# Casts at the beginning, norm 2's plain product and the products of the end, rearranged in a decoder block kernel

## The chip, the cores and the metric

The kernel runs on one core of a Trainium2 chip. The metric is device microseconds of one execution: the median of 3 runs of the kernel before is 800.8 us (800.53 to 800.96). One more execution was profiled.

## What is computed

A decoder block on 512 tokens of 1024 channels, in float32. Two token mixers, a causal convolution and a recurrence, are merged by gates; a channel mixer follows. Cut to what the change touches:

```python
h = rmsnorm(x, norm1_g)                     # norm 1
z = h @ w_in + b_in                         # 1024 -> 6656 columns
...
x = x + m @ w_mix_out
h = rmsnorm(x, norm2_g)                     # norm 2
x = x + (silu(h @ ffn_w1) * (h @ ffn_w3)) @ ffn_w2
return rmsnorm(x, norm_f_g)                 # final norm
```

## The kernel before

Every product of two float32 matrices is made of three matmuls of a rounded type: each operand is split into a high part (a cast) and a low part (the operand less its high part), and high x high, high x low and low x high are added up. `split_to` (line 114) makes such a pair: line 123 the cast, line 119 the subtraction. Weights come in chunks of 128x1024: `emit_chunk` (line 145) issues the load on SP's queue (`raw_in` for w_in), casts on ScalarE, and subtracts on GpSimd or VectorE into `hl_in`. Tokens are split into two halves, LO and HI, of 256.

The program has four engines with orders of their own. In the block of lines 595 to 618 the order of TensorE, ScalarE, VectorE and SP is that of the code; elsewhere a scheduler picks it, within the limits that `tc.issue_after` sets. On each engine, instructions run in that order.

**Beginning.** TensorE first runs WARM products of a matrix of ones (line 495). Of x, each of four token tiles t has two column halves; `norm1_rows(t)` squares them on ScalarE (lines 539, 545), takes the root (546) and the reciprocal (547), and scales x on VectorE (579). The small per-channel parameters are loaded as rows (`load_rows`) and transposed into `par` (`rows_turned`, line 507, and a copy, 508). `turn_half("tx", ...)` transposes a token half of x on TensorE (563), ScalarE casts it, scaled by the norm's gain, to the high parts h10h to h17h (566), and VectorE makes the low parts h10l to h17l (567). `early_mm(i, half)` multiplies four chunks of weights, numbers 0, 8, 1 and 9 of w_in (the first to fourth that are loaded), by these (`mm3`, line 523, tile z).

**Norm 2.** `turn_half("th", ...)` does the same for h20 to h27. Token half LO is turned early, and the products fr of it run meanwhile (`f_product`, line 1060). Then half HI is turned (the four th pieces around 472 us), and the plain products of the feed-forward network, f1 and f3 of column blocks 0 and 11, run over all 512 tokens (`mm3`, line 523, tile f). `ffn_out` takes silu of f1 (ScalarE, line 1051, tile si) and multiplies by f3 (VectorE, line 1052, ou and ov). All other blocks go through a scheme with seven products instead of eight, for which sums of weights are formed (VectorE, line 351, tile raw_fb; GpSimd stores them by DMA, line 349, and SP loads them, line 339), and sums of h2: `full` (line 1067) adds a high and a low part to h2f (VectorE, line 886, tile hf), and `f_inputs` makes hs from it. `f_out` (line 1115) ends a block: silu on ScalarE (line 1117, with a table load), and a product on VectorE (1118).

**End.** `out_end` (line 1199) finishes four token tiles. `finish` (line 1181) takes the root of the mean square (`rstd_begin`, `rstd_end`, tiles jk) and scales by it and by the gain gf to `of`, two DMAs for each tile. For the last two tiles a lambda, `third`, makes the last products (tile or, line 933).

## Time and profile before

| | us |
| --- | --- |
| median of 3 runs | 800.8 |
| profiled execution, its own time | 800.93 |
| its span in the trace | 799.2 |
| TensorE busy | 788.9 |
| VectorE busy | 675.5 |
| ScalarE busy | 472.1 |
| GpSimd busy | 231.6 |

In the profile PE is TensorE's matmuls, DVE is VectorE, ACT is ScalarE, POOL is GpSimd and SP the engine that issues most DMAs. A row gives a start, a length, the engine, the line of the kernel, the operation, output and inputs, shape and count; in square brackets stands how long the engine had been idle and what ended that. A 512-column matmul is 0.39 us long on its own, but pipelined ones start closer together, so what one costs is read from start to start.

### The profile page before, as it was taken

The numbers are of one execution on the slowest core, as the hardware profiler recorded it, in microseconds if no ns is written. First come the engines' busy times: TensorE is split into PE (matmuls) and PEld (weight loads), VectorE is DVE, ScalarE is ACT, GpSimd is POOL, SyncE is SP. The second block draws the span as 40 slices with busy tenths as digits, with TensorE's granted clock in tenths as the row PEclk, the third lists the DMA queues.
The fourth block names the chain that finished last, engine by engine and source line by source line (L and its number), as shares of the span: only waits on it lengthen the run. The fifth ranks groups of instructions, "written<-read, shape, count | busy, mean of one in ns | idle before, by whom it ended". The sixth has DMA issues, their size and how long they took to land.

```text
span 799.2 us, 12191 instructions
## 1 busy us (share of the span) xinstructions
PE 788.9 (99%) x4374; PEld 689.5 (86%) x4374; DVE 675.5 (85%) x1027; ACT 472.1 (59%) x678; POOL 231.6 (29%) x182
## 2 busy tenths in 40 slices
PE   8999999999999999999999999999999999999997
PEld 7988888888888888888888888999999999888885
DVE  4699899999989988796787889978778887889756
ACT  7546595898668855563335574545455555577443
POOL 3565867687766855130000000000000000000000
PEclk9999999999999999999999999999999999999999
DMA  7945647378564754468947536477555553676552
GB/s 212 239 122 165 174 150 212 121 213 237 164 193 144 225 177 125 128 193 266 282 153 246 172 107 183 120 178 190 147 132 133 133 132 106 205 265 203 198 172 105
DMA packets 184624, 140.29 MB, mean 176 GB/s; under 512 B 14279, under 2 KB 162163, under 8 KB 184563
## 3 DMA queue, kind: packets, MB, share of 16 engines
q1 hardware_dynamic: 183123, 134.27, 55.4%
q0 software_dynamic: 1440, 5.24, 3.5%
q8 instruction: 34, 0.56, 0.3%
q14 instruction: 27, 0.22, 0.1%
HBM read 113.79 MB, written 18.64 MB: 166 GB/s over the span
## 4 chain that ended last, share of the span: by engine, by line
PE 91%; DVE 4%; DMA 2%; ACT 2%; issue 1%; SPq 0%; DVEq 0%; POOLq 0%; ACTq 0%
PE z L523 35%; PE or L933 13%; PE ft L1060 7%; PE yb L523 7%; PE fa L1060 6%; PE ya L523 5%; PE mxr L933 5%; PE fe L1060 3%; PE g L807 3%; PE fr L1060 3%; PE fb L1060 2%; PE f L523 1%; DMA raw_fb<-in_ffn_w_dram 1%; DMA raw_fb<-raw_fb 1%; DMA x<-in_x_dram 1%
## 5 line engine op out<-in xcount | busy, mean ns | idle before, releaser
L682 DVE SCALAR_TENSOR_TENSOR cv<-u,par,cv 128x511 f32<-128x511 f32 (+16 forms) x240 | 162.0, 728 | 2.3 <-ACT cv L679 2.2
L119 POOL TENSOR_TENSOR hl_in<-raw_in,hl_in 128x1024 fp32r<-128x1024 f32 x52 | 125.9, 2426 | 82.8 <-ACT hl_in L123 80.4
L349 POOL DMA_DIRECT2D raw_fb<-raw_fb x10 | 8.7, 874 | 299.3 <-DVE raw_fb L351 186.6
L119 POOL TENSOR_TENSOR ows<-ows 128x256 f32<-128x256 f32 x66 | 57.2, 870 | 37.5 <-DMA ows<-in_ffn_w_dram 34.5
L123 ACT CAST hl_in<-raw_in 128x1024 fp32r<-128x1024 f32 x52 | 54.2, 1043 | 10.2 <-PE z L523 6.5
L123 ACT CAST hl_ft<-raw_fb 128x1024 fp32r<-128x1024 f32 x40 | 41.8, 1048 | 28.9 <-DVE raw_fb L351 12.7
L119 DVE TENSOR_TENSOR hl_ft<-raw_fb,hl_ft 128x1024 fp32r<-128x1024 f32 x40 | 48.6, 1219 | 9.7 <-ACT hl_ft L123 9.6
L119 DVE TENSOR_TENSOR hl_fb<-raw_fb,hl_fb 128x1024 fp32r<-128x1024 f32 x30 | 36.6, 1220 | 9.2 <-ACT hl_fb L123 8.9
L523 PE MATMUL z<-h10h,hl_in 128*128 128x512 f32 (+1 forms) x112 | 42.2, 378 | 1.0 <-DVE h10l L567 1.0
L523 PE MATMUL z<-h13h,hl_in 128*128 128x512 f32 (+1 forms) x112 | 41.7, 374 | 0.0
L523 PE MATMUL z<-h14h,hl_in 128*128 128x512 f32 (+1 forms) x112 | 41.7, 374 | 0.0
L523 PE MATMUL z<-h15h,hl_in 128*128 128x512 f32 (+1 forms) x112 | 41.7, 374 | 0.0
L523 PE MATMUL z<-h11h,hl_in 128*128 128x512 f32 (+1 forms) x112 | 41.7, 374 | 0.0
L523 PE MATMUL z<-h16h,hl_in 128*128 128x512 f32 (+1 forms) x112 | 41.7, 374 | 0.0
L523 PE MATMUL z<-h17h,hl_in 128*128 128x512 f32 (+1 forms) x112 | 41.7, 374 | 0.0
L523 PE MATMUL z<-h12h,hl_in 128*128 128x512 f32 (+1 forms) x112 | 41.7, 374 | 0.0
L351 DVE TENSOR_TENSOR raw_fb<-raw_fb,raw_fb 128x1024 f32<-128x1024 f32 x20 | 24.5, 1225 | 16.9 <-DMA raw_fb<-in_ffn_w_dram 16.6
L119 DVE TENSOR_TENSOR hl_ob<-raw_ob,hl_ob 128x1024 fp32r<-128x1024 f32 (+1 forms) x23 | 27.0, 1172 | 10.5 <-ACT hl_ob L123 7.6
L123 ACT CAST hl_ob<-raw_ob 128x1024 fp32r<-128x1024 f32 (+1 forms) x23 | 23.4, 1016 | 20.7 <-PE or L933 14.7
L123 ACT CAST hl_fb<-raw_fb 128x1024 fp32r<-128x1024 f32 x30 | 31.4, 1047 | 6.7 <-PE mxr L933 3.7
L1060 PE MATMUL fe<-hs_0h,hl_ft 128*128 128x256 f32 x160 | 30.8, 284 | 0.4 <-DVE hl_ft L119 0.4
L1060 PE MATMUL ft<-hs_1h,hl_ft 128*128 128x256 f32 x160 | 30.4, 283 | 0.0
(965 smaller groups left out, 2610.1 us busy)
## 6 DMA issues: line engine op xcount, KB each, us to landing
raw_in<-in_w_in_dram SPq DMA_DIRECT2D x52, 512.0 KB
raw_fb<-in_ffn_w_dram SPq DMA_DIRECT2D x96, 256.0 KB
ows<-in_ffn_w_dram SPq DMA_DIRECT2D x44, 256.0 KB
os<-ows SPq DMA_DIRECT2D x22, 512.0 KB
raw_ob<-in_ffn_w_dram SPq DMA_DIRECT2D x33, 256.0 KB
raw_ot<-os SPq DMA_DIRECT2D x33, 256.0 KB
raw_lo<-in_lru_w_out_dram SPq DMA_DIRECT2D x16, 320.0 KB
raw_fb<-raw_fb POOLq DMA_DIRECT2D x10, 512.0 KB, 4.5
```

Of the source, the lines that this page charges most:

```text
L119: return eng.tensor_tensor(out=o, in0=x, in1=y, op=ALU.subtract)
L123: copy(h, full)
L349: pool_e.dma_start(out=q, in_=y, accum_op=ALU.add)
L351: vec.tensor_tensor(out=q, in0=q, in1=y, op=ALU.add)
L523: pe.matmul(ps, l, r, start=i == 0, stop=i == n - 1)
L682: vec.scalar_tensor_tensor(out=acc[c][:, s:], in0=u[c][:, : T - s], scalar=dw(c, s), in1=acc[c][:, s:], op0=ALU.mult, op1=ALU.add)
L807: pe.matmul(ps, l, r, start=k == 0, stop=k == len(mms) - 1)
L933: pe.matmul(banks[i], l_[:, ts], r_, start=start and n == 0, stop=stop and n == 2, skip_group_check=again)
L1060: pe.matmul(ps[:, HALVES[i]], lw[:, 4 * i + c, :], rx_, start=not (again or i or c or m), stop=bool(i and c == 3 and m == 2), skip_group_c ...
```

## The change

At the beginning, WARM goes from 12 to 21; the first four chunks of weights are cast by VectorE (`vec.tensor_copy`) instead of ScalarE; the second chunk's cast comes behind the low parts of the first half on VectorE, and the third's and fourth's ahead of the second half's; the parameter rows other than norm 1's gains are loaded behind x, and turned later, in a matrix of rows of their own.

At norm 2, the token half HI is turned in four portions of two pieces. ScalarE first copies a piece to h2f (scaled, in full), then casts that, and VectorE subtracts; the additions of `full` for HI go. Behind each portion stands a quarter of the plain product f1 of block 0: LO with rows 0 to 3 of h2, LO with 4 to 7, then HI likewise, in matmuls of 256 columns. The f3 of that block makes its low parts last. `f_out` of the first blocks waits until the last copy to h2f has been issued.

At the end, `finish` is split: `finish_begin` makes the square of x2's second half and its product with the gain for both of the last two tiles ahead of the last products; the scaling of that product goes to VectorE for all but the very last tile.

```diff
--- before.py
+++ after.py
@@ -34,7 +34,7 @@
 RAW = 4
 HL = 5
 AHEAD = 4
-WARM = 12
+WARM = 21
 
 FEW, MANY = 32, 112
 
@@ -128,11 +128,11 @@
             last = sub(eng, l, full, h.bitcast(F32))
         if eng is pool_e:
             newest["sub"] = last.ins
-        return h, l
+        return h, l, last
 
     def split(name, full, eng, p_=None, copy=act.copy):
         p_ = p_ or pairt(name)
-        return split_to(*p_, full, eng, copy)
+        return split_to(*p_, full, eng, copy)[:2]
 
 
     chunks = []
@@ -142,7 +142,7 @@
     def wchunk(key, src, kt, cols, where="hl", lo=pool_e, after=None):
         chunks.append((key, src, kt, cols, where, lo, after))
 
-    def emit_chunk():
+    def emit_chunk(copy=act.copy):
         if emitted[0] == GATES_AT:
             load_gates()
         key, src, kt, cols, where, lo, after = chunks[emitted[0]]
@@ -161,7 +161,7 @@
             newest["load"] = nc.sync.dma_start(rv.rearrange("p (k n) -> p k n", k=kt), src).ins
         if where != "long":
             hl = hls.tile([P, 2, 1024], F32R, tag="hl", name=f"hl_{key}")
-            h, l = split_to(hl[:, 0, :n], hl[:, 1, :n], rv, lo)
+            h, l, _ = split_to(hl[:, 0, :n], hl[:, 1, :n], rv, lo, copy)
             if after:
                 after(rv, h)
             held[key] = (h.rearrange("p (k n) -> p k n", k=kt), l.rearrange("p (k n) -> p k n", k=kt))
@@ -171,9 +171,9 @@
                 for i in range(2)
             ]
 
-    def emit_to(n):
+    def emit_to(n, copy=act.copy):
         while emitted[0] < min(len(chunks), n):
-            emit_chunk()
+            emit_chunk(copy)
 
     def weights(key, ahead=AHEAD):
         i = next(i for i, c in enumerate(chunks) if c[0] == key)
@@ -452,7 +452,12 @@
     n_rows = sum(n for _, n in ROWS)
     n_first = ROWS[0][1] + ROWS[1][1]
     par = consts.tile([P, n_rows], F32, name="par")
-    row_at = lambda c: (0, c) if c < n_first else (1 + (c - n_first) // P, (c - n_first) % P)
+    starts = (0, ROWS[0][1], n_first)
+
+    def row_at(c):
+        b = sum(c >= s_ for s_ in starts) - 1
+        return b + (c - starts[b]) // P, (c - starts[b]) % P
+
     at, col, parts = 0, {}, []
     for name, n in ROWS:
         col[name] = at
@@ -497,8 +502,7 @@
     first = [i for i, (lo, _, _) in enumerate(parts) if lo < n_first]
     load_x(0)
     load_x(1)
-    for i in first:
-        load_rows(i)
+    load_rows(first[0])
 
     def rows_turned(c0, c1):
         pt = bank2(f"par_ps{c0}")
@@ -553,7 +557,7 @@
             between()
         return rstd_end(begun, halves[1], junk[1])
 
-    def turn_half(name, rows, gname, dest, hf, bk, some=range(ND)):
+    def turn_half(name, rows, gname, dest, hf, bk, some=range(ND), full=None):
 
         cs = slice(hf * 256, hf * 256 + 256)
         for c in some:
@@ -563,6 +567,11 @@
                 pe.transpose(ps[:, t * P : (t + 1) * P], src, ident)
             g = pc(gname, c)
             h, l = (v[:, cs] for v in dest[c])
+            if full:
+                f = full[c][:, cs]
+                newest["half"] = act.activation(f, ps[:, :256], AF.Copy, scale=g).ins
+                _, _, last = split_to(h, l, f, vec)
+                continue
             act.activation(h, ps[:, :256], AF.Copy, scale=g)
             last = vec.scalar_tensor_tensor(out=l, in0=ps[:, :256], scalar=g, in1=h.bitcast(F32), op0=ALU.mult, op1=ALU.subtract)
         return last.ins
@@ -595,24 +604,26 @@
     with tc.manual_schedule(engines={ET.PE, ET.Activation, ET.DVE, ET.SP}):
         norm1_rows(0)
         norm1_rows(1)
-        rows_turned(0, n_first)
-        emit_to(1)
+        rows_turned(0, ROWS[0][1])
+        emit_to(1, vec.tensor_copy)
         turn_half("tx", xt, "norm1_g", h1p, 0, [bank, bank, bank, bank2])
-        emit_to(2)
+        emit_to(2, vec.tensor_copy)
         load_x(2)
         load_x(3)
+        for i in first[1:]:
+            load_rows(i)
         norm1_rows(2)
         norm1_rows(3)
-        emit_to(3)
+        emit_to(4, vec.tensor_copy)
         for i in range(len(parts)):
             if i not in first:
                 load_rows(i)
         early_mm(0, 0)
         early_mm(1, 0)
         turn_half("tx", xt, "norm1_g", h1p, 1, [bank2, bank, bank])
-        emit_to(4)
         early_mm(2, 0)
         early_mm(3, 0)
+        rows_turned(ROWS[0][1], n_first)
         rows_turned(n_first, n_rows)
         for i in range(4):
             early_mm(i, 1)
@@ -1073,8 +1084,17 @@
 
     for c in range(ND):
         full(c, LO)
-    turned = turn_half("th", xs, "norm2_g", h2p, 1, [bank2])
     h2 = parts_of(h2p)
+    plain_1 = bank(f"f1_{PLAIN}")
+    with tc.manual_schedule(engines={ET.PE}):
+        ws = w_tiles(f"f1_{PLAIN}", ND, 0)
+        for q in range(4):
+            cs, ks = HALVES[q // 2], range(4 * (q % 2), 4 * (q % 2) + 4)
+            turned = turn_half("th", xs, "norm2_g", h2p, 1, [bank2], range(2 * q, 2 * q + 2), h2f)
+            for k in ks:
+                (wh, wl), (xh, xl) = ws[k], (v[:, cs] for v in h2[k])
+                for m, (l, r) in enumerate(((wh, xh), (wh, xl), (wl, xh))):
+                    pe.matmul(plain_1[:, cs], l, r, start=k == 0 and m == 0, stop=k == ND - 1 and m == 2)
     with tc.issue_after(turned):
         emit_to(emitted[0] + 3)
 
@@ -1083,8 +1103,6 @@
     def f_inputs(ks):
         for k in ks:
             a1, a2 = h2f[k], h2f[k + 4]
-            full(k, HI)
-            full(k + 4, HI)
             g = [longt(f"hs{k}_{i}") for i in range(2)]
             s1, s2, s3, s4 = (v[:, cs] for v in g for cs in HALVES)
             sub(vec, s1, a2[:, HI], a1[:, HI])
@@ -1110,7 +1128,8 @@
 
     def ended(k, c11, r2):
         add(c11, r2, c11)
-        f_out(c11, o7.uv[k][0][:, LO])
+        with tc.issue_after(newest["half"]):
+            f_out(c11, o7.uv[k][0][:, LO])
 
     def f_out(c, dst, sign=1.0):
         s_ = shortt("sl")
@@ -1120,9 +1139,10 @@
     for k in FIRST:
         ended(k, begun(k, first[k][0]), first[k][1])
     for i, j in enumerate((PLAIN, PLAIN + KF)):
-        p1, p3 = bank(f"f1_{j}"), bank(f"f3_{j}")
-        mm3(p1, w_tiles(f"f1_{j}", ND), h2)
-        mm3(p3, w_tiles(f"f3_{j}", ND), h2)
+        p1, p3 = bank(f"f1_{j}") if i else plain_1, bank(f"f3_{j}")
+        if i:
+            mm3(p1, w_tiles(f"f1_{j}", ND), h2)
+        mm3(p3, w_tiles(f"f3_{j}", ND), h2, lo_last=not i)
         ffn_out(j, p1, p3)
         if i == 0:
             f_inputs(range(2, 4))
@@ -1178,21 +1198,22 @@
         for h in range(2):
             nc.sync.dma_start(gf[h], a["norm_f_g"][h * T : (h + 1) * T].partition_broadcast(P))
 
-    def finish(t, ps=None, rest=None):
+    def finish_begin(t):
 
         o = [longt(f"of{t}{i}") for i in range(2)]
         jk = [bank(f"jk{t}{i}") for i in range(2)]
-        first = x2[t][0] if ps is None else ps
         begun = rstd_begin(x2[t][1], jk[0])
-        if rest:
-            vec.tensor_tensor(out=o[1], in0=x2[t][1], in1=gf[1], op=ALU.mult)
-            rest()
-        r = rstd_end(begun, first, jk[1])
+        vec.tensor_tensor(out=o[1], in0=x2[t][1], in1=gf[1], op=ALU.mult)
+        return o, jk[1], begun
+
+    def finish(t, o, jk, begun, first):
+
+        r = rstd_end(begun, first, jk)
         vec.scalar_tensor_tensor(out=o[0], in0=first, scalar=r, in1=gf[0], op0=ALU.mult, op1=ALU.mult)
-        if rest:
+        if t == NT - 1:
             act.activation(o[1], o[1], AF.Copy, scale=r)
         else:
-            vec.scalar_tensor_tensor(out=o[1], in0=x2[t][1], scalar=r, in1=gf[1], op0=ALU.mult, op1=ALU.mult)
+            vec.tensor_scalar(out=o[1], in0=o[1], scalar1=r, scalar2=None, op0=ALU.mult)
         for i in (0, 1):
             nc.sync.dma_start(o_nat[:, t, i * T : (i + 1) * T], o[i])
 
@@ -1215,12 +1236,14 @@
                     seed = add(r1[i], r1[i], x2[2 + i][0])
                     if i == 0:
                         newest["tie"] = seed.ins
-        finish(0)
+        finish(0, *finish_begin(0), x2[0][0])
         for k in range(kh - hold, kh):
             outq.get(k, "t4")
-        finish(1)
+        finish(1, *finish_begin(1), x2[1][0])
+        begun = [finish_begin(2 + i) for i in range(2)]
         for i in range(2):
-            finish(2 + i, r1[i], lambda: third(i, range(kh - hold, kh)))
+            third(i, range(kh - hold, kh))
+            finish(2 + i, *begun[i], r1[i])
 
     o7.run(x2, loads, out_end)
 
```

On VectorE, in the beginning, from the last low part of the first half to the first of the second (x_117 to x_121 are the column halves of the token tiles 2 and 3, stats the norm's numbers; hl_in is a chunk of weights). Before:

```order
L567 TENSOR_SCALAR h17l<-tx_233,par,h17h 128x256
L540 TENSOR_SCALAR stats<-stats 128x1
L547 RECIPROCAL stats<-stats 128x1
L579 TENSOR_SCALAR x_117<-x_117,stats 128x512
L579 TENSOR_SCALAR x_118<-x_118,stats 128x512
L540 TENSOR_SCALAR stats<-stats 128x1
L547 RECIPROCAL stats<-stats 128x1
L579 TENSOR_SCALAR x_119<-x_119,stats 128x512
L579 TENSOR_SCALAR x_120<-x_120,stats 128x512
L567 TENSOR_SCALAR h10l<-tx_333,par,h10h 128x256
```

and in the change, beginning right behind h17l:

```order
L123 COPY hl_in_249<-raw_in_247 128x1024
L544 TENSOR_SCALAR stats<-stats 128x1
L551 RECIPROCAL stats<-stats 128x1
L588 TENSOR_SCALAR x_118<-x_118,stats 128x512
L588 TENSOR_SCALAR x_119<-x_119,stats 128x512
L544 TENSOR_SCALAR stats<-stats 128x1
L551 RECIPROCAL stats<-stats 128x1
L588 TENSOR_SCALAR x_120<-x_120,stats 128x512
L588 TENSOR_SCALAR x_121<-x_121,stats 128x512
L123 COPY hl_in_277<-raw_in_275 128x1024
L123 COPY hl_in_282<-raw_in_280 128x1024
L576 TENSOR_SCALAR h10l<-tx_348,par,h10h 128x256
```

The cast of the second chunk now stands behind h17l and ahead of x's scaling, and those of the third and fourth stand between the last x and h10l.

On TensorE at norm 2, behind the fr products (th are transposes, f_0 and f_11 the plain products of blocks 0 and 11). Before, all of it from the first transpose on:

```order
L563 MATMUL th_4467<-ident,xs_4216 128x128
L563 MATMUL th_4467<-ident,xs_4218 128x128
L563 MATMUL th_4472<-ident,xs_4216 128x128
L563 MATMUL th_4472<-ident,xs_4218 128x128
L523 MATMUL f_0_4570<-h20h,hl_f_0_4509 128x512
L523 MATMUL f_0_4571<-h20h,hl_f_0_4514 128x512
L523 MATMUL f_11_4675<-h20h,hl_f_11_4519 128x512
L563 MATMUL th_4477<-ident,xs_4216 128x128
L563 MATMUL th_4477<-ident,xs_4218 128x128
L523 MATMUL f_0_4570<-h20l,hl_f_0_4509 128x512
```

and in the change, from the last matmuls of the first quarter through the second portion of transposes:

```order
L1097 MATMUL f_0_4480<-h22h,hl_f_0_4485 128x256
L1097 MATMUL f_0_4480<-h23h,hl_f_0_4485 128x256
L1097 MATMUL f_0_4480<-h23l,hl_f_0_4485 128x256
L1097 MATMUL f_0_4480<-h23h,hl_f_0_4485 128x256
L567 MATMUL th_4512<-ident,xs_4229 128x128
L567 MATMUL th_4512<-ident,xs_4231 128x128
L567 MATMUL th_4518<-ident,xs_4229 128x128
L567 MATMUL th_4518<-ident,xs_4231 128x128
L1097 MATMUL f_0_4480<-h24h,hl_f_0_4485 128x256
L1097 MATMUL f_0_4480<-h24l,hl_f_0_4485 128x256
```

The products between the portions of transposes are now ones of 256 columns with the half that was turned before; those of 512 columns come later.

On ScalarE at the same place (fr and c belong to the seven-product scheme). Before:

```order
L1107 COPY c_1_4554<-fr_1_4359 128x512
L123 COPY hl_f_11_4574<-raw_f_11_4572 128x1024
L1117 ACT_TABLE_LOAD
L1117 ACTIVATE sl<-c_1_4554 128x256
L566 ACTIVATE h20h<-th_4467,par 128x256
L566 ACTIVATE h21h<-th_4472,par 128x256
L1107 COPY c_2_4562<-fr_2_4409 128x512
L566 ACTIVATE h22h<-th_4477,par 128x256
L566 ACTIVATE h23h<-th_4482,par 128x256
L1117 ACTIVATE sl<-c_2_4562 128x256
```

and in the change:

```order
L1125 COPY c_1_4628<-fr_1_4372 128x512
L123 COPY hl_f_11_4597<-raw_f_11_4595 128x1024
L123 COPY hl_fb_3_4648<-raw_fb_3_4645 128x1024
L572 ACTIVATE hf_3986<-th_4488,par 128x256
L572 ACTIVATE hf_3987<-th_4494,par 128x256
L123 COPY h20h<-hf_3986 128x256
L123 COPY h21h<-hf_3987 128x256
L572 ACTIVATE hf_3988<-th_4512,par 128x256
L572 ACTIVATE hf_3989<-th_4518,par 128x256
```

The table load and silu (line 1117, now 1136) no longer stand among the turned pieces, each of which takes two operations, and the cast of hl_fb_3 stands ahead of all of them.

On ScalarE at the end (jk are the squares, or the last two products). Before:

```order
L539 ACTIVATE jk_7886,stats<-x2b_7002 128x512
L123 COPY hl_ot_10_7831<-raw_ot_10_7829 128x512
L546 ACTIVATE stats<-stats 128x1 x2
L545 ACTIVATE jk_7887,stats<-or_7007 128x512
L539 ACTIVATE jk_7909,stats<-x2b_7004 128x512
L546 ACTIVATE stats<-stats 128x1
L1193 ACTIVATE of_7885<-of_7885,stats 128x512
L545 ACTIVATE jk_7910,stats<-or_7008 128x512
L546 ACTIVATE stats<-stats 128x1
L1193 ACTIVATE of_7908<-of_7908,stats 128x512
```

and in the change:

```order
L543 ACTIVATE jk_7928,stats<-x2b_7042 128x512
L123 COPY hl_ot_10_7871<-raw_ot_10_7869 128x512
L543 ACTIVATE jk_7935,stats<-x2b_7044 128x512
L550 ACTIVATE stats<-stats 128x1 x2
L549 ACTIVATE jk_7929,stats<-or_7047 128x512
L550 ACTIVATE stats<-stats 128x1
L549 ACTIVATE jk_7936,stats<-or_7048 128x512
L550 ACTIVATE stats<-stats 128x1
L1214 ACTIVATE of_7934<-of_7934,stats 128x512
```

The square of x2b_7004, now x2b_7044, and the scaling of the third tile's `of` have left the place between the squares of the two tiles or.

## The prediction

> **What bounds the kernel now.** I began with the busy times and the chain of work that ended last, on the page.
>
> ```profile
> PE 788.9 (99%) x4374; PEld 689.5 (86%) x4374; DVE 675.5 (85%) x1027; ACT 472.1 (59%) x678; POOL 231.6 (29%) x182
> ...
> PE 91%; DVE 4%; DMA 2%; ACT 2%; issue 1%; SPq 0%; DVEq 0%; POOLq 0%; ACTq 0%
> ```
>
> TensorE is busy for 788.9 of 799.2 us and carries 91% of the chain. So an edit is worth only what it takes from TensorE's waits, and a product that grows costs its full length. I therefore asked next for everything that TensorE waits for; columns are total, times, longest.
>
> ```profile
> PE z L523 <- DVE h10l L567: 1.0, 1, 1.0
> PE tx L563 <- DVE x L579: 0.9, 2, 0.6
> PE fe L1060 <- DVE hl_ft L119: 0.4, 1, 0.4
> PE f L523 <- ACT h20h L566: 0.4, 1, 0.4
> ```
>
> The first two are at the beginning, the last two around norm 2. These, and the tail behind the last matmul, are all that the three parts of the change can win. The profiled execution took 800.93 us with a span of 799.2 us; I make the sum against 800.93, which is 0.13 above the median of 800.8.
>
> **Beginning.** TensorE's timeline (start, length) for the first 21 us:
>
> ```profile
> 1.08 5.49 PE L495 MATMUL warm<-ones 128*128 128x128 f32 x24 [1.08 <-DVE ones L488]
> ...
> 8.18 1.86 PE L563 MATMUL tx<-ident,x 128*128 128x128 f32 x15 [0.64 <-DVE x L579]
> ...
> 11.08 0.38 PE L523 MATMUL z<-h10h,hl_in 128*128 128x256 f32 x1 [1.04 <-DVE h10l L567]
> ...
> 18.40 2.24 PE L563 MATMUL tx<-ident,x 128*128 128x128 f32 x15 [0.26 <-DVE x L579]
> 20.60 0.39 PE L523 MATMUL z<-h10h,hl_in 128*128 128x256 f32 x1
> ```
>
> The 12 warm-up products are 24 records at 5.49/24 = 0.229 us; the transposes from 8.18 on, of the same shape, take 1.86/15 = 0.124. So the rate nearly doubles somewhere between 6.57 and 8.18. With 21 products (42 records) the warm-up ends at 6.57 + 18 x 0.124 = 8.8 if that comes at 6.57, and at 8.18 + 11 x 0.124 = 9.5 if at 8.18 (31 records are through by then). I take 9.0.
>
> The Trainium skill ("TensorE: Matmul & The Clock Gate", Part 1: The HAM clock gate) says that the array runs at half rate until it has been busy for one window of about 3.4 us, whatever is issued, and that the window runs freely. With a release at 1.08 + 3.4 the warm-up would end at about 7.7 and the sum below would be some 0.3 us lower, an estimate from that page; the row of 24 slow records up to 6.57 disagrees with so early a release.
>
> The other engines there:
>
> ```profile
> 9.09 1.05 ACT L123 CAST hl_in<-raw_in 128x1024 fp32r<-128x1024 f32 x1 [1.69 <-DMA raw_in<-in_w_in_dram]
> ...
> 10.54 0.48 DVE L567 SCALAR_TENSOR_TENSOR h10l<-tx,par,h10h 128x256 fp32r<-128x256 f32 x1 [1.90 <-ACT h10h L566]
> ...
> 13.29 0.47 DVE L567 SCALAR_TENSOR_TENSOR h17l<-tx,par,h17h 128x256 fp32r<-128x256 f32 x1
> ...
> 15.79 1.38 DVE L579 TENSOR_SCALAR x<-x,stats 128x512 f32<-128x512 f32 x2
> ...
> 17.86 0.88 DVE L579 TENSOR_SCALAR x<-x,stats 128x512 f32<-128x512 f32 x2
> 19.27 0.48 DVE L567 SCALAR_TENSOR_TENSOR h10l<-tx,par,h10h 128x256 fp32r<-128x256 f32 x1 [0.53 <-ACT h10h L566]
> ...
> 14.08 2.41 POOL L119 TENSOR_TENSOR hl_in<-raw_in,hl_in 128x1024 fp32r<-128x1024 f32 x1 [1.48 <-ACT hl_in L123]
> ```
>
> Before, ScalarE's cast of the first weights (9.09, when they land) stood ahead of h10h, and so of h10l and z. The changed kernel has it on VectorE. No row shows a 128x1024 cast there; these are the nearest:
>
> ```profile
> L219 DVE CAST hl_gate<-raw_gate x6: 283/283/805, 54.8 to 227.0; 32x256 fp32r<-32x256 f32 x6
> ...
> L119 DVE TENSOR_TENSOR hl_ft<-raw_fb,hl_ft 128x1024 fp32r<-128x1024 f32 x40 | 48.6, 1219 | 9.7 <-ACT hl_ft L123 9.6
> ...
> 226.97 0.81 DVE L219 CAST hl_gate<-raw_gate 32x256 fp32r<-32x256 f32 x1 [0.58 <-POOL hl_gate L119]
> ...
> 226.89 0.73 POOL L119 TENSOR_TENSOR ows<-ows 128x256 f32<-128x256 f32 x1
> ```
>
> The upper end is 1.22, a difference of that size; the lower is 0.28, the cast of a quarter of the columns. Per column a cast costs less than a difference (0.28 for 256 columns, against 0.42 for the product of two operands at 497.84, quoted with norm 2), so between 0.28 and 1.22 I take 0.68, with 0.60 until the next operation starts.
>
> Step by step: the warm-up ends at 9.0; the row of norm gains and the first two transposes follow, VectorE copies the gains (9.3 to 9.45), casts (until 10.05) and makes h10l at about 10.07 instead of 10.54. z starts 0.54 behind h10l, as before: 10.6 instead of 11.08. The eight low parts end at 13.3 instead of 13.76, the second cast, now behind them on VectorE, at 13.9, and GpSimd's low part of it runs from 13.9 to 16.3.
>
> Here comes the catch. The x at 15.79 is slow: two take 1.38, where the pair at 17.86 takes 0.88. The first of them ends only 0.28 behind GpSimd's operation (14.08 + 2.41 = 16.49), and the cast at 226.97 likewise ends 0.16 behind the GpSimd operation of 226.89 to 227.62 and took 0.81 instead of 0.28. So x cannot pass GpSimd's low part, in the change either: it ends at about 16.6 instead of 16.77, and the last x, hence tx at 18.40, is only 0.17 earlier.
>
> The Trainium skill ("SBUF — State Buffer", the part on the shared port pair) has this as an exclusive lock between VectorE's two-port operations and GpSimd, held for a whole instruction. It speaks against this change, which puts four more such operations on VectorE; the two rows above agree with it.
>
> Then the next two casts (third and fourth weights) stand on VectorE between the last x and h10l of the second half: 2 x 0.60. VectorE comes free of x at about 18.5, so h10l is at 19.7, not 19.27: 0.43 late. z of the third weights waits for a PSUM bank that the third low part frees, so it starts at 21.03 instead of 20.60. GpSimd has both low parts done by 24, earlier than before, which gives back about 0.15; the table of rows is now turned in four pieces here instead of three, 0.1. **Beginning: +0.35** (from -0.9, if x is not held, to +1.7, both casts at 1.22 and 0.5 more on the way to h10l). The row loads now behind x2 and x3 on SP's queue are not needed before 26 us; this hides them.
>
> **Norm 2.** Timelines of TensorE, then ScalarE, then VectorE:
>
> ```profile
> 472.07 0.60 PE L563 MATMUL th<-ident,xs 128*128 128x128 f32 x4
> 473.03 0.96 PE L523 MATMUL f<-h20h,hl_f 128*128 128x512 f32 x3 [0.36 <-ACT h20h L566]
> ...
> 477.98 0.39 PE L523 MATMUL f<-h23h,hl_f 128*128 128x512 f32 x1
> 478.21 0.40 PE L523 MATMUL f<-h24h,hl_f 128*128 128x512 f32 x1
> 478.75 0.83 PE L563 MATMUL th<-ident,xs 128*128 128x128 f32 x4
> ...
> 514.23 0.28 PE L1060 MATMUL fe<-hs_0h,hl_ft 128*128 128x256 f32 x1
> 514.35 0.28 PE L1060 MATMUL fe<-hs_0l,hl_ft 128*128 128x256 f32 x1
> 515.04 0.50 PE L1060 MATMUL fe<-hs_0h,hl_ft 128*128 128x256 f32 x2 [0.41 <-DVE hl_ft L119]
> ...
> 470.91 1.28 ACT L1117 ACT_TABLE_LOAD   x1
> ...
> 472.52 0.46 ACT L566 ACTIVATE h20h<-th,par 128x256 fp32r<-128x256 f32 x1
> 472.88 0.47 ACT L566 ACTIVATE h21h<-th,par 128x256 fp32r<-128x256 f32 x1
> ...
> 497.21 0.60 ACT L1051 ACTIVATE si<-f 128x512 f32<-128x512 f32 x1 [2.98 <-PE f L523]
> ...
> 497.84 0.42 DVE L1052 TENSOR_TENSOR ou<-si,f 128x256 f32<-128x256 f32 x1
> ```
>
> Four transposes at 0.11 would end at 472.51, but f starts at 473.03, because h20h waits behind the table load: 0.52 lost. At 478.21 a matmul of 512 columns takes 0.54 to the next start instead of 0.23: 0.31 lost. In the change TensorE has products of the first token half (which is long ready) behind each four transposes, so both waits go: -0.83. It has 48 halves at 0.12 (514.23 to 514.35) instead of 24 wholes at 0.23 (477.98 to 478.21): +0.24. Against that, ScalarE now makes two operations of each piece, a copy and a cast, and VectorE a subtraction. No row shows that; ScalarE's nearest is h20h, 0.36 from start to start. From 472.07, four transposes (0.44) and twelve halves (1.44) three times over put the last four transposes at 477.71 to 478.15; two copies and the cast h26h then end at 479.4 (0.15 + 0.36 + 0.36 + 0.36, and 0.1 until its end is seen), h26l at 479.85. TensorE has six halves (0.72), two wholes (0.46) and four more matmuls (0.5) until it wants h26l at about 479.7: +0.2. **So TensorE is 0.4 earlier** behind the plain products (0.83 - 0.24 - 0.2).
>
> The stall at 514.35 (0.69 instead of 0.12, 0.57 lost) ends a chain back through hl_ft, a DMA and VectorE to ou at 497.84, which stood behind si (497.21 + 0.60 = 497.81). There the product that si reads was the last of four. In the change it comes 24 matmuls before the last, so ou waits only for the last product's end, at 496.7: 1.14 earlier. TensorE comes 0.4 earlier and the data 1.14 earlier, so the stall is gone, with 0.17 to spare. The eight additions that VectorE no longer makes (0.33 each) keep it from becoming the new wait. **Norm 2: -1.0** (from +0.3, where ScalarE's 16 steps at their full 0.47 make the last pieces 0.7 later and the wait at 514 stays, to -1.6, where nothing of the 0.2 is lost and the smaller gaps at each transpose go too).
>
> **End.**
>
> ```profile
> 790.81 0.39 PE L933 MATMUL or<-hl_ot,ovb10l 128*128 128x512 f32 x1
> 791.24 0.58 ACT L545 ACTIVATE jk<-or 128x512 f32<-128x512 f32 x1 [4.48 <-PE or L933]
> 792.85 0.39 PE L933 MATMUL or<-hl_ot,ovb10l 128*128 128x512 f32 x1
> 792.95 0.72 ACT L1193 ACTIVATE of<-of,stats 128x512 f32<-128x512 f32 x1 [0.23 <-DVE stats L547]
> 793.58 0.58 ACT L545 ACTIVATE jk<-or 128x512 f32<-128x512 f32 x1
> ```
>
> The third token tile's squares start 0.43 behind its last matmul (790.81 to 791.24). The fourth's start 0.73 behind (792.85 to 793.58), because `of` at 792.95 is ahead of them on ScalarE. In the change that scaling goes to VectorE and x2b's squares are done before, so the fourth can start at 793.28. **End: -0.3** (0 to -0.35). The products made ahead lie on VectorE beside the last matmuls; without that cover one costs about 0.6, as one is 128x512.
>
> **Sum:** +0.35 - 1.0 - 0.3 = -0.95, that is 800.0 for the profiled execution and 799.85 beside the median, which I give as 799.8.
>
> **The rivals.**
> - **Late beginning** (slower than before). If the slow rate of the warm-up does not end with it, 42 x 0.229 puts its end at 10.7: 1.7 later than taken. The path from there to h10l, the casts, GpSimd's low part and x then moves whole: beginning +2.05, total +0.75, 801.55. It decides from a warm-up end of about 9.95, where the beginning costs the 1.3 that the other parts win. The transposes from 8.18 speak against it. A cast of 1.22 ends in the same place: 801.2. Together 0.15.
> - **x is not held**, since GpSimd's operation now starts at another point: the first x ends at 15.0, tx follows the products at 17.4, z is 1 us earlier, beginning -0.9: 798.6. The two held rows speak against it: 0.10.
> - **The wait at 514 stays**, since DMA queues or VectorE and not si set it: 0.6 less won, 800.4. VectorE's 85% speaks for it: 0.15.
> - **Early clock.** If the warm-up ends by 8.5, the landing at 9.09 binds: cast until 9.69, h10l 0.3 earlier than taken, beginning about 0: 799.5. The row of 24 slow records speaks against it: 0.05. (This is what a release after one window of the page named above would do.)
> - **Norm 2 wins more** (-1.6) and the two casts cost little, total about -1.9: 798.9. What speaks for it is that TensorE's starts at 478.75 to 479.3 are spread wider than 0.11 (four transposes in 0.83): 0.13.
>
> **How the numbers follow.** The forecast, 799.8 with a range of its own of 799.1 to 800.5, has 0.42. A measurement here can tell about 0.2%, 1.6 us, from no change: faster is below 799.2, slower above 802.4. Faster: 0.10 + 0.13 + 0.11 of the forecast's own low end = 0.34. Slower needs the late beginning together with the wait at 514 or slow casts: 0.10. The rest, 0.56, is within. The range 797.9 to 802.2 reaches from x not held with the other parts at their best (-0.9 - 1.6 - 0.35) to the late beginning with 0.6 not won at 514.
>
> **What would show it.** In the changed profile: warm x42 ending near 9.0; casts of 0.68 on VectorE; z from 10.6; one x held until GpSimd's end near 16.3; z of the third weights at 21.0; no gap above 0.2 between the transposes and products of norm 2; ou just behind the last f; no wait of fe near 514; the last jk 0.43 behind the last matmul. A warm-up past 10, an x of 0.48 beside a GpSimd operation, or fe still waiting would make the prediction wrong.

## The result and the profile after

In runs of both kernels beside each other the changed kernel has a median of 800.23 us (799.09 to 801.25, 22 runs) against 801.44 us (800.25 to 802.74, 22 runs): a ratio of 0.9984, 95% interval 0.9977 to 0.9991, which is 0.7 to 1.8 us faster, 1.3 in the middle. The forecast was 0.95 faster. The prediction took 1.6 us as the least that a measurement here can tell; with 22 runs of each kernel a gain of 1.3 us can be told from none. The profiled execution of the changed kernel, however, took 800.75 us with a span of 799.0, hardly less than the 800.93 and 799.2 of before. So this case has two questions: whether the three parts did what the forecast says, and where this one execution lost what the medians show.

First the changed kernel's list of what TensorE waited for, behind its start (total, times, longest):

```profile
PE fr L1071 <- ACT ft L1171: 0.6, 1, 0.6
PE tx L567 <- DVE h10l L576: 0.6, 1, 0.6
PE tx L567 <- DVE x L588: 0.5, 1, 0.5
PE or L944 <- DVE x2b L897: 0.2, 1, 0.2
```

The wait for h20h, which stood in the list before, is gone, and so is that for hl_ft (fe) as a wait of the list; 0.23 us of it are left, as the rows at 514 below show. The wait of the first z for h10l is gone too. New are a wait of the transposes for h10l, a wait of fr for ft, and one of or for x2b. The last two lie at 543 and 736 us, where nothing was changed.

**Beginning**, TensorE, then VectorE, then GpSimd of the changed kernel:

```profile
1.09 7.19 PE L500 MATMUL warm<-ones 128*128 128x128 f32 x42 [1.09 <-DVE ones L493]
...
10.18 0.36 PE L527 MATMUL z<-h10h,hl_in 128*128 128x256 f32 x1
...
17.79 1.42 PE L567 MATMUL tx<-ident,x 128*128 128x128 f32 x11 [0.52 <-DVE x L588]
...
8.90 0.68 DVE L123 CAST hl_in<-raw_in 128x1024 fp32r<-128x1024 f32 x1
9.58 0.48 DVE L576 SCALAR_TENSOR_TENSOR h10l<-tx,par,h10h 128x256 fp32r<-128x256 f32 x1
...
14.09 2.48 DVE L588 TENSOR_SCALAR x<-x,stats 128x512 f32<-128x512 f32 x2
...
18.05 1.29 DVE L123 CAST hl_in<-raw_in 128x1024 fp32r<-128x1024 f32 x2
19.25 0.48 DVE L576 SCALAR_TENSOR_TENSOR h10l<-tx,par,h10h 128x256 fp32r<-128x256 f32 x1
...
13.49 2.40 POOL L119 TENSOR_TENSOR hl_in<-raw_in,hl_in 128x1024 fp32r<-128x1024 f32 x1 [1.44 <-DVE stats L544]
```

z starts at 10.18, 0.9 earlier than before. A 128x1024 cast on VectorE takes 0.68, as estimated. But the pair of x at 14.09 takes 2.48, where it took 1.38 before and a pair takes 0.88 with nothing beside it; it stands beside GpSimd's low part (13.49 to 15.89). And two casts, 1.29 together, stand ahead of the second h10l, which at 19.25 is where it was before (19.27).

The table of parameter rows, now turned in four pieces, costs more than it did. TensorE in the changed kernel, and then in the kernel before:

```profile
26.52 0.73 PE L511 MATMUL par_ps<-ident,rows 52*128 52x52 f32 x4
27.01 0.36 PE L527 MATMUL z<-h10h,hl_in 128*128 128x256 f32 x1
...
26.59 0.48 PE L507 MATMUL par_ps<-ident,rows 128*128 128x128 f32 x3
26.84 0.36 PE L523 MATMUL z<-h10h,hl_in 128*128 128x256 f32 x1
```

From the start of the last z ahead of the rows (26.31, and 26.47 before) to the first z behind them it is 0.70 us instead of 0.37.

**Norm 2**, TensorE around the first portion of transposes, the last plain product and the former wait near 514, then ScalarE and VectorE around the last plain product:

```profile
472.25 0.60 PE L567 MATMUL th<-ident,xs 128*128 128x128 f32 x4
472.60 0.36 PE L1097 MATMUL f<-h20h,hl_f 128*128 128x256 f32 x1
...
496.07 0.39 PE L527 MATMUL f<-h27h,hl_f 128*128 128x512 f32 x1
...
513.68 0.28 PE L1071 MATMUL fe<-hs_0l,hl_ft 128*128 128x256 f32 x1
514.03 0.51 PE L1071 MATMUL fe<-hs_0h,hl_ft 128*128 128x256 f32 x2
...
495.00 0.60 ACT L1062 ACTIVATE si<-f 128x512 f32<-128x512 f32 x1 [1.86 <-DVE ou L1137]
...
496.56 0.42 DVE L1063 TENSOR_TENSOR ou<-si,f 128x256 f32<-128x256 f32 x1
...
499.64 1.22 DVE L351 TENSOR_TENSOR raw_fb<-raw_fb,raw_fb 128x1024 f32<-128x1024 f32 x1
```

From the start of four transposes to the next product it is now 0.35 us, where 0.96 stood before (472.07 to 473.03). silu begins at 495.0, before the last plain product ends, and no longer behind it. ou starts 0.49 behind the start of the last f, instead of 1.11 (496.73 to 497.84), and the sum of weights (line 351) 3.57 behind it. At 513.68 fe takes 0.35 to the next start where 0.12 is usual: 0.23 lost, instead of 0.57.

**End**, ScalarE and TensorE:

```profile
792.98 0.39 PE L944 MATMUL or<-hl_ot,ovb10l 128*128 128x512 f32 x1
...
793.40 0.58 ACT L549 ACTIVATE jk<-or 128x512 f32<-128x512 f32 x1 [1.02 <-PE or L944]
```

The last squares start 0.42 behind the last matmul, instead of 0.73.

**Where this execution lost it.** The last matmul starts at 792.98, 0.13 later than before, though TensorE was 1.0 us earlier at 515. Two rows of the changed kernel tell where TensorE waited:

```profile
543.43 0.39 PE L1071 MATMUL fr<-hs_1h,hl_fb 128*128 128x256 f32 x1 [0.59 <-ACT ft L1171]
...
736.07 0.73 PE L944 MATMUL or<-hl_ot,ovb0h 128*128 128x512 f32 x2 [0.18 <-DVE x2b L897]
```

and the chain of work behind the first (start, length, what):

```profile
523.27 6.73 DMA raw_fb<-in_ffn_w_dram
...
540.54 1.23 DVE raw_fb L351
...
541.84 1.05 ACT hl_ft L123
542.89 0.49 ACT ft L1171
```

ScalarE's copy ft stands behind a cast that waits for a sum of weights (540.54). Further back in the same chain an earlier sum waited for a load that took 6.73 us; VectorE stood still for it for 1.00:

```profile
530.12 1.23 DVE L351 TENSOR_TENSOR raw_fb<-raw_fb,raw_fb 128x1024 f32<-128x1024 f32 x1 [1.00 <-DMA raw_fb<-in_ffn_w_dram]
```

In the kernel before, the sum at this place (529.48) follows without such a wait. Whether that belongs to the change or to this execution is what the experiments had to tell.

### The profile page after: what moved, and what is told of

Its sections match the earlier page's. It is cut to its first block, busy times and chain, and to the rows that moved or that the text cites. A ratio compares the mean times of both kernels' runs of the same rounds, so it can differ in the third digit from the quotient of the medians.

```text
span 799.0 us, 12275 instructions
## 1 busy us (share of the span) xinstructions
PE 790.3 (99%) x4417; PEld 692.8 (87%) x4417; DVE 676.4 (85%) x1027; ACT 469.8 (59%) x681; POOL 232.1 (29%) x182
## 4 chain that ended last, share of the span: by engine, by line
PE 85%; DVE 6%; DMA 6%; issue 1%; SPq 1%; ACT 1%; DVEq 0%; POOLq 0%; ACTq 0%
PE z L527 35%; PE or L944 7%; PE yb L527 7%; PE fa L1071 6%; PE ft L1071 6%; PE ya L527 5%; PE mxr L944 5%; PE g L818 3%; PE fr L1071 3%; PE fe L1071 3%; PE fb L1071 2%; DMA raw_fb<-in_ffn_w_dram 2%; DMA raw_fb<-raw_fb 2%; PE f L527 1%; DVE hl_ob L119 1%
## 5 line engine op out<-in xcount | busy, mean ns | idle before, releaser
L123 ACT CAST hl_in<-raw_in 128x1024 fp32r<-128x1024 f32 x48 | 50.0, 1041 | 10.7 <-PE z L527 6.6
```

Source lines behind the costliest of these rows:

```text
L123: copy(h, full)
```

## The experiments

For all of them I cut the trace into stages at TensorE's starts: the first z behind the table of rows; the first transpose of norm 2's second half; the last plain product f; the first fr behind fe; the last matmul; and the start of VectorE's last product. Lengths in us, worked out from the rows at these places:

| kernel | to z behind rows | to th | to last f | to fr | to last matmul | to the end |
| --- | --- | --- | --- | --- | --- | --- |
| before | 26.84 | 445.23 | 24.66 | 18.88 | 277.23 | 1.98 |
| changed | 27.01 | 445.23 | 23.82 | 18.54 | 278.37 | 1.67 |
| e1, beginning alone | 27.13 | 445.50 | 24.91 | 18.79 | 277.54 | 1.98 |
| e2, norm 2 alone | 26.43 | 445.24 | 23.97 | 19.08 | 277.31 | 1.98 |
| e3, end alone | 26.38 | 445.60 | 24.97 | 18.95 | 277.25 | 1.67 |
| e5 | 26.72 | 445.96 | 23.81 | 18.38 | 277.32 | 1.67 |
| e6 | 26.87 | 445.23 | 23.81 | 18.39 | 277.33 | 1.67 |
| e7 | 26.85 | 445.47 | 24.07 | 18.39 | 277.33 | 1.67 |
| e8, norm 2 and end | 26.43 | 445.32 | 23.87 | 18.38 | 277.48 | 1.67 |
| e9 | 27.58 | 445.24 | 23.81 | 18.52 | 277.31 | 1.67 |
| e10 | 26.13 | 445.23 | 23.81 | 18.38 | 277.36 | 1.67 |

Ratios below are to the kernel before in runs beside it on the same chip.

**e1, e2, e3: each part alone.** Edits: the hunks of the diff at the beginning, at norm 2, and at the end, each put into the kernel before; for instance, for the end,

```diff
-        for i in range(2):
-            finish(2 + i, r1[i], lambda: third(i, range(kh - hold, kh)))
+        begun = [finish_begin(2 + i) for i in range(2)]
+        for i in range(2):
+            third(i, range(kh - hold, kh))
+            finish(2 + i, *begun[i], r1[i])
```

> The kernel before with the part at the beginning alone. My theory (what the two traces show: z starts 0.9 us earlier, but x is held behind GpSimd and the third and fourth cast delay h10l of the second half, so that TensorE is level again by 27 us): no gain, -0.2 to +0.2 us against the kernel before, and in the trace z from about 10.2, tx of the second half about 17.8, z of the third weights about 20.5. Rival (the whole gain of the change, 1.3 us, comes from here, and the trace hides it): -0.8 to -1.3 us.

Measured: 1.0002 (0.9993 to 1.0011), 801.87 against 801.56 us. No gain that the times can tell (-0.6 to +0.9 us); z at 10.30, the second tx at 17.9, z of the third weights at 20.7. Against the four executions in the table with the old beginning (26.38 to 26.84, mean 26.52) the three with the new one (27.01, 27.13, 27.58, mean 27.24) are 0.7 us later. A fifth with the old beginning, e11, is at 26.79, still ahead of all three.

> The kernel before with the part at norm 2 alone. My theory: -0.8 to -1.2 us; in the trace TensorE is 1.0 to 1.2 us earlier than in the kernel before just behind fe near 514 us, and what is lost again later depends on how long the DMAs of the weight sums take in that execution. Rival (VectorE, without a pause from 715 to 736 us in both kernels, or the chain of DMAs, sets the time there, so what norm 2 wins is always given back): 0 to -0.3 us, with a wait of TensorE for ft near 543 or for x2b near 736 us as large as the gain.

Measured: 0.9978 (0.9968 to 0.9988), 1.8 us faster (1.0 to 2.6), more than the whole change. The rival falls: from fr to the last matmul it took 277.31, so nothing was given back there. But the trace is not what was expected at fr: from th to fr TensorE gained only 0.5 on the kernel before, not 1.0 to 1.2, because fe waited in this execution, and longer than before the change (0.88 from 513.26 to 514.14, so 0.76 lost, against 0.57). The sum of weights started 3.57 behind the last f, as in the changed kernel; it is the load behind it that was late, 4.23 us where the kernel before has 3.46 at this step of the chain. e2, and then the kernel before:

```profile
506.17 4.23 DMA raw_fb<-in_ffn_w_dram
...
507.84 3.46 DMA raw_fb<-in_ffn_w_dram
```

> The kernel before with the part at the end alone. My theory: -0.3 us, with the last squares 0.43 us behind the last matmul instead of 0.73. Rival (something else, such as the output DMAs, ends the program): 0, with the last DMA issue no closer to the last matmul than before.

Measured: 0.9999 (0.9990 to 1.0007). The times can't tell 0.3 from 0. The trace can: the last stage is 1.67 in all eight executions in the table with this part and 1.98 in all three without.

**e5: the third and fourth casts back on ScalarE.**

```diff
         norm1_rows(3)
-        emit_to(4, vec.tensor_copy)
+        emit_to(3)
...
         turn_half("tx", xt, "norm1_g", h1p, 1, [bank2, bank, bank])
+        emit_to(4)
```

> The changed kernel with the casts of the third and fourth weights back on ScalarE (third ahead of the second half's high parts, fourth behind them), all else as changed. My theory (these two casts on VectorE are what keeps the beginning from gaining): h10l of the second half 0.6 us earlier (18.65 instead of 19.25), z of the third weights about 19.9 instead of 20.5, TensorE about 0.5 us earlier from 27 us on; time 0.3 to 0.6 us below the changed kernel. Rival (x, held by GpSimd, or the PSUM bank alone sets z): z of the third weights stays at 20.5 and the time is that of the changed kernel. It is also a second look at the changed kernel behind 27 us: if the wait for ft near 543 us is the change's doing, it is here too with 0.5 us or more; if it is the DMAs of that one execution, it is gone or of another size.

Measured: 0.9987 (0.9978 to 0.9995), in its time not apart from the changed kernel. In the trace the second h10l comes 1.42 us behind the last pair of x instead of 2.00:

```profile
17.54 0.88 DVE L588 TENSOR_SCALAR x<-x,stats 128x512 f32<-128x512 f32 x2
18.96 0.48 DVE L576 SCALAR_TENSOR_TENSOR h10l<-tx,par,h10h 128x256 fp32r<-128x256 f32 x1 [0.53 <-ACT h10h L575]
```

That is the 0.6 of the two casts. Half of it was lost to a warm-up that here took 7.71 instead of 7.19, so z of the third weights was at 20.28. And the stage from fr to the last matmul was 277.32: the wait near 543 was not there.

**e4: GpSimd's third low part right behind the second.** The third and fourth casts are on ScalarE, as in e5, but `emit_to(3)` stands between `norm1_rows(2)` and `norm1_rows(3)`, and `emit_to(4)` right behind the latter.

> One look. The changed kernel with the third and fourth casts on ScalarE, the third so early (ahead of the fourth token tile's norm) that GpSimd makes the third low part right behind the second. My theory (a GpSimd operation holds VectorE's scaling of x for its whole length): the first pair of x is held as before (2.5 us), and now the second pair too, until GpSimd's third low part ends near 18.3 us: 1.5 us or more instead of 0.88, tx of the second half at about 18.6 instead of 17.8 to 18.1, though ScalarE and VectorE have less to do there than in the changed kernel. Rival (the first pair is slow for a reason of its own): the second pair takes 0.88 us and tx is at 17.8 to 18.1.

Measured: 802.47 in a single run. VectorE and GpSimd; the first row of VectorE is the first x of the pair by itself:

```profile
13.88 2.09 DVE L588 TENSOR_SCALAR x<-x,stats 128x512 f32<-128x512 f32 x1
...
13.88 4.60 DVE L588 TENSOR_SCALAR x<-x,stats 128x512 f32<-128x512 f32 x2
...
13.28 4.92 POOL L119 TENSOR_TENSOR hl_in<-raw_in,hl_in 128x1024 fp32r<-128x1024 f32 x2 [1.54 <-DVE stats L544]
```

and all eight x by their form (shortest, median, longest in ns; first and last start):

```profile
L588 DVE TENSOR_SCALAR x<-x,stats x8: 479/486/2586, 5.7 to 19.6; 128x512 f32<-128x512 f32 x8
```

Not the second pair was held, as I wrote, but the first, and each x of it by one of GpSimd's operations: the first took 2.09 us, until 15.97, and the second, the longest of the eight, 2.59, until 18.48, which is 0.28 behind GpSimd's end at 18.20. Together they took 4.60, where 0.88 is their plain time. tx started at 19.71. So here x is held until GpSimd's operation beside it has ended: a pair loses 1.6 us with one low part beside it (2.48), 3.7 with two.

**e6: the second low part on VectorE, late.** On e5: instead of GpSimd right behind the cast, VectorE makes it between the scalings of the third and the fourth token tile.

```diff
...
         norm1_rows(2)
+        vec.tensor_tensor(**waiting.pop())
         norm1_rows(3)
```

> The kernel with the casts of the third and fourth weights on ScalarE, and with the low part of the second weights on VectorE, between the scalings of the third and the fourth token tile, instead of on GpSimd. My theory (x is held by GpSimd's low part, and that is the next thing that sets the beginning): the pair of x scalings takes 0.88 us instead of 2.48, tx of the second half starts near 17.25 instead of 17.8 to 18.1, z of the third weights near 19.4 instead of 20.3 to 20.6, and TensorE is past the table of rows at about 25.8 instead of 26.7 to 27.1. Time 0.6 to 1.2 us below the changed kernel, 2 us below the kernel before. Rival (x at that place is slow of itself, because its data or its scalar come late): the pair still takes over 1.3 us and nothing is won.

Measured: 0.9980 (0.9972 to 0.9989). The pair of x takes its plain time:

```profile
14.36 0.88 DVE L588 TENSOR_SCALAR x<-x,stats 128x512 f32<-128x512 f32 x2
```

z of the third weights was at 19.80 (19.4 was expected), but TensorE was past the rows only at 26.87 (25.8 was expected), because it met a new wait:

```profile
25.23 0.38 PE L527 MATMUL z<-h10h,hl_in 128*128 128x256 f32 x1 [0.30 <-POOL hl_in L119]
```

The fourth low part, whose weights are loaded behind the parameter rows in this kernel, had become late.

**e7: 12 warm-up products.**

```diff
-WARM = 21
+WARM = 12
```

> The changed kernel with 12 warm-up products instead of 21. My theory (with 21 the warm-up itself ends between 7.8 and 8.8 us, depending on when the faster rate sets in, and now stands ahead of the first transposes; with 12 TensorE was at the fast rate by 8.2 all the same): z starts no later than in the changed kernel (10.1 to 10.6), 15 transposes still take 1.9 us; time -0.2 to +0.1 us against the changed kernel. Rival (the nine more are needed: with 12 the pause of TensorE between 6.6 and 8.5 puts off the fast rate): the transposes take over 3 us and z starts 0.5 to 1 us later; time +0.5 us or more.

Measured: 0.9979 (0.9970 to 0.9987); z at 9.97 and 1.86 us for 15 transposes. In this execution the nine more products were not needed. But two other executions with 12, e8 and e10, show the rival's case: 15 transposes took 3.06 and 3.32. TensorE in e8, by row and by stretch (busy, granted clock, DMA share, GB/s):

```profile
8.45 3.06 PE L563 MATMUL tx<-ident,x 128*128 128x128 f32 x15 [0.76 <-DVE x L584]
...
5.00:8.40 3.40, 1.62 (x10) 1.00 1.13 311
8.40:11.50 3.10, 3.06 (x16) 0.58 1.06 362
```

After a stretch in which TensorE was busy for 1.62 of 3.40 us, the granted clock was 0.58. (The column cannot be read for the warm-up itself: it shows 1.00 there in every execution, also while a record took 0.229 instead of 0.124.) With 21 products no execution shows that, with 12 two of seven (the kernel before, e2, e3, e7, e8, e10, e11). No cost of it shows later, since x sets the second half: z of the third weights was at 19.90 and 19.69, earlier than in every other execution but e6 (19.80).

**e8: norm 2 and end, with the old beginning.**

> The kernel before with the parts at norm 2 and at the end, without the part at the beginning. My theory (the part at the beginning costs about 0.4 us: TensorE past the table of rows at 27.0 and 27.1 with it, at 26.8, 26.4 and 26.4 without): 0.2 to 0.6 us below the changed kernel, 1.5 to 2 us below the kernel before. Rival (the beginning gains, since z starts earlier): above the changed kernel by 0.3 us or more.

Measured: 0.9973 (0.9963 to 0.9982), 799.46 against 801.59 us, 2.1 us faster. The changed kernel's 0.9984 lies just outside this interval, but its own (0.9977 to 0.9991) overlaps it: that the beginning of the change costs is shown by the stages, not by the times.

**e9: silu's product last.**

```diff
-            mm3(p1, w_tiles(f"f1_{j}", ND), h2)
-        mm3(p3, w_tiles(f"f3_{j}", ND), h2, lo_last=not i)
+            w1t, w3t = w_tiles(f"f1_{j}", ND), w_tiles(f"f3_{j}", ND)
+            mm3(p3, w3t, h2)
+            mm3(p1, w1t, h2)
...
```

> The changed kernel, but in the plain products of block 11 the one that silu reads is made last, as in the kernel before, and not second to last. My theory (half of what norm 2 wins comes from silu no longer standing between the last plain product and VectorE's chain to fe): VectorE's ou begins about 0.85 us behind the end of the last f matmul instead of 0.35, and fe waits 0.4 to 0.6 us longer near 514 us; time +0.4 to +0.6 us against the changed kernel. Rival (the DMAs of the sums alone set the wait at 514): ou moves, but the wait at 514 stays between 0.2 and 0.4 us and the time is that of the changed kernel.

Measured: 0.9988 (0.9979 to 0.9996), which is the changed kernel's. ou moved as expected: 1.10 behind the start of the last f instead of 0.49. But fe lost 0.20 near 514, no more than in the changed kernel's trace, and the sum of weights came only 0.27 later, 3.84 behind the last f. That is what the rival said, but the run does not isolate silu's place. VectorE from ou to the sum, in e9 and then in the kernel before:

```profile
497.39 0.41 DVE L1111 SCALAR_TENSOR_TENSOR hs<-hs,hf 128x256 f32<-128x256 f32 x1
497.73 0.42 DVE L1063 TENSOR_TENSOR ou<-si,f 128x256 f32<-128x256 f32 x1
...
500.47 1.22 DVE L351 TENSOR_TENSOR raw_fb<-raw_fb,raw_fb 128x1024 f32<-128x1024 f32 x1
...
497.84 0.42 DVE L1052 TENSOR_TENSOR ou<-si,f 128x256 f32<-128x256 f32 x1
498.18 0.42 DVE L1093 SCALAR_TENSOR_TENSOR hs<-hs,hf 128x256 f32<-128x256 f32 x1
...
500.92 1.22 DVE L351 TENSOR_TENSOR raw_fb<-raw_fb,raw_fb 128x1024 f32<-128x1024 f32 x1
```

In e9 the scheduler put one operation for hs, which stands behind ou before the change, ahead of it, so ou and the sum are 2.74 apart; in the kernel before and in the changed kernel they are 3.08 apart. So the 0.62 by which the changed kernel's sum is earlier (3.57 behind the last f instead of 4.19) is all ou's place, and e9 won 0.35 of it in another way.

What fe loses follows the sum's place in nine of the eleven executions in the table: 0.48 to 0.63 where the sum is 4.19 behind the last f (the kernel before, e1, e3), 0.20 at 3.84 (e9), at most 0.08 at 3.57 (e5, e6, e7, e8, e10). The other two, also at 3.57, are the changed kernel (0.23) and e2 (0.76).

**e11: the product left whole**, on e8. All transposes stand ahead of it again, and block 0's low parts come in the old order.

```diff
-            turned = turn_half("th", xs, "norm2_g", h2p, 1, [bank2], range(2 * q, 2 * q + 2), h2f)
...
+    turned = turn_half("th", xs, "norm2_g", h2p, 1, [bank2], range(ND), h2f)
```

> The kernel with norm 2 and end, but with the plain product of block 0 left whole (512 columns, behind all the transposes, as before the change), while ScalarE still copies each piece in full and then casts it, and VectorE no longer adds. My theory (the win at norm 2 comes from work that stands between the transposes, that is from the halved product): TensorE waits 1.2 us or more between 472 and 480 us, and the time is 0.8 to 1.5 us above the kernel with norm 2 and end. Rival (it comes from VectorE, which is rid of eight additions, and so reaches the sums of weights earlier): the time stays within 0.4 us of that kernel, and fe near 514 us waits no more than there.

Measured: 1.0077 (1.0059 to 1.0094), 6 us slower than before, far beyond both. It is not in the table, since the products behind f come in another order. TensorE stood still for 3.1 us:

```profile
479.59 0.50 PE L523 MATMUL f<-h20h,hl_f 128*128 128x512 f32 x1 [3.12 <-DVE hl_f L119]
```

The stage from th to the last f took 29.48, against 23.87 in e8. What TensorE waited for here is the low parts of the weights, which the scheduler put behind all the pieces on VectorE, so this does not isolate the halved product. It shows that copies in full, with the whole product in the order that the scheduler then makes, lose; it does not show what the relief of eight additions is worth by itself. How the win divides between the halves and the scheduler's order stays open.

**e10: the finds together.** e6, with 12 warm-up products and the fourth weights loaded ahead of the parameter rows (cast and low part where e6 has them).

> The changed kernel's norm 2 and end, with a beginning that takes the finds together: 12 warm-up products, first and second cast on VectorE, third and fourth on ScalarE, the second low part on VectorE late, the fourth weights loaded ahead of the parameter rows. My theory: pair of x 0.88 us, z of the third weights near 19.5, no wait for the fourth low part (0.5 us in the run with the second low part on VectorE), TensorE past the table of rows near 26.0; time 0.3 to 0.6 us below the kernel with norm 2 and end alone, 2.3 to 2.7 us below the kernel before. Rival (the beginning is bounded by the landing of the weights and by TensorE's own 26 us of work, so nothing more is to be had there): past the table of rows no earlier than 26.4, time that of norm 2 and end alone.

Measured: 0.9965 (0.9952 to 0.9977), 798.68 against 801.73 us: the fastest of all, 2.8 us below the kernel before (1.8 to 3.8). TensorE was past the rows at 26.13, against 26.43 in e8, and without a wait for the fourth low part. From the changed kernel (0.9984, 0.9977 to 0.9991) the interval is apart but for its rim; from e8 its time is not, so that the mended beginning gains is seen in one trace alone.

## Why the prediction was right, and where not

The direction and the size hold: -0.95 forecast, -1.3 measured (-0.7 to -1.8). By the means of the stages in the table, the parts that the change touches give +0.7 - 1.0 - 0.4 - 0.3 = -1.0. That the sum comes out so close is in part luck: the beginning cost 0.35 more than forecast, and norm 2 won 0.35 more.

- **What bounds the kernel.** Right: between 27 and 472 us, and from fr on, the stages keep their length (445.2 to 446.0; 277.2 to 277.5 but for one execution).
- **Beginning**, +0.35 forecast, +0.7 by the traces. The mechanism was right at each step: the cast at 0.68, z earlier, x held until 0.28 behind GpSimd's end, and the two casts ahead of the second h10l. e4 and e6 show the hold, e5 the two casts. Two things made the size wrong. The term for the table of rows was 0.1, and it is 0.33 (0.70 instead of 0.37). And the execution that I subtracted from was late: its first weights were cast at 9.09, those of e2, e3 and e8, with the same beginning, at 8.78, 8.57 and 8.39. Against the mean of these four, z of the third weights is 0.58 later (20.80 in the mean of the changed kernel, e1 and e9, against 20.21), where 0.43 was forecast.
- **Early clock** (a rival, 0.05). Its condition came true: the warm-up ended at 8.28, not 9.0, and by 8.5 in four of the six executions with 21 products. Its consequence did not. The landing did not bind (the cast ran from 8.90), and every step came 0.4 to 0.5 earlier than taken: h10l at 9.58 and not 10.07, the second h10l at 19.25 (19.82 in e9) and not 19.7, z of the third weights at 20.57 and not 21.03. Even so the beginning did not come out level: in the changed kernel's trace TensorE was past the rows at 27.01, later than in any of the five with the old beginning. In the working of the warm-up, 42 records with a release at 1.08 + 3.4 would end at 7.8 by the rates given there, not at 7.7.
- **Norm 2**, -1.0 forecast, -1.35 by the traces. Up to the last f it was -0.4 forecast and -0.98 found (23.87 in the mean of eight executions against 24.85 in three). The waits of 0.52 and 0.31 went, and h26l came as late as expected (it ended at 479.87; 479.85 was expected). Left out of the sum, though in the low end of its range, were the small losses where transposes and products change: six of 0.08 to 0.12 before, four of 0.08 in the change, and 0.23 among the four transposes at 478.75. For the wait at 514, -0.57 was forecast, -0.4 found in the mean, and -0.5 where no DMA was late. The step as described holds: ou and the sum are 0.62 earlier behind the last f.
- **The wait at 514 stays** (a rival, 0.15, and a sign of being wrong in the prediction's own list). It came true in e2, where fe lost 0.76 with the sum in its new place, and in part in the changed kernel's trace (0.23). In five executions it is gone. e2's chain shows a late load; so the DMAs can bring the wait back, but seldom did.
- **Norm 2 wins more** (a rival, 0.13). Its first half came near, -1.35 of the -1.6; its second, that the two casts cost little, did not.
- **End**, -0.3 forecast, -0.31 found, the step as described.
- **The profiled execution of the changed kernel** lost 1.1 us from fr to the last matmul (278.37), which none of the other ten in the table did, seven of which have the change at norm 2 too. In none of these ten did the sum that waited 1.00 at 530.12 wait for its load. So it is that execution's DMAs and not the change, as far as seven can tell; why that load was late is not shown.

## What to carry to other kernels

In this case one profiled execution carried tenths of a microsecond, once a whole one, of its own at places where a DMA's landing sets the time; before a forecast of 0.1% is built on a row, the same stretch should be read in a second execution. Work moved to another engine has to be followed to the next thing that engine owes: here two casts that ScalarE had time for went ahead of the low parts that TensorE waits for, and, with the hold of x by GpSimd, gave back what the first cast had won. An experiment that moves one thing in a scheduled program has to be read for what else moved: e9 and e11 each changed VectorE's order as well. Where a program of short waits is bounded by one engine, cutting it into stages at that engine's starts tells parts of 0.3 us apart that eleven timed runs cannot.

## What the runs showed of the hardware

- The hold of VectorE by GpSimd: a scaling of 128x512 takes 0.48 us by itself and took 2.09 and 2.59 beside a low part of GpSimd that ran when it started. That an operation of 0.48 can be held five times its length, and twice in a row, was more than I had reckoned with. The Trainium skill ("SBUF — State Buffer", the part on the shared port pair) has a lock for one whole instruction, by which the other engine waits until it ends; the rows of e4, one hold for each of GpSimd's operations, agree with it. The 0.28 that x still takes behind GpSimd's end is less than its own 0.48.
- The start of the fast rate moved: 42 warm-up records took 6.67 to 7.71 us in six executions, 24 took 5.49 in five and 5.03 and 4.66 in two. And it fell back: in e11, after a pause of 3.1 us, TensorE first ran on at 0.23 us for a matmul of 512 columns and then slowed to 0.43 for 3.2 us. Its stretches (busy, granted clock, DMA share, GB/s) and two rows:

```profile
479.60:481.00 1.40, 1.40 (x6) 1.00 0.09 22
481.00:484.20 3.20, 3.20 (x10) 0.50 0.89 259
484.20:487.00 2.80, 2.80 (x13) 0.96 1.12 308
...
481.56 0.63 PE L523 MATMUL f<-h23h,hl_f 128*128 128x512 f32 x1
481.99 0.63 PE L523 MATMUL f<-h23l,hl_f 128*128 128x512 f32 x1
```

The Trainium skill ("TensorE: Matmul & The Clock Gate", Part 1: The HAM clock gate) describes a freely running window of about 3.4 us after which the clock is halved or given in full; the halving (0.50) and, roughly, the length (3.2 us) agree with these rows. The slow stretch begins 1.4 us after work has come back, not with it.
